# Differential attention on one core: the group's output copy moves from ScalarE to VectorE, and two row buffers become one

## The chip, the core and the metric

One core of a Trainium2 chip runs the whole kernel. A core has five engines that work through queues of their own, each in its order: TensorE (PE in the profile; its weight loads are PEld), VectorE (DVE), ScalarE (ACT), GpSimd (POOL) and SyncE (SP, which here only issues DMA transfers). An instruction that must wait for another engine holds up everything behind it in its own queue. The metric is the device time of one execution in microseconds; lower is better.

## The reference

One layer of a hybrid diffusion backbone: a modulated norm, one input projection into queries, keys, values and Fourier channels, then attention on one half of the heads and Fourier mixing on the other, an output projection, and an MLP. What this case touches is the differential attention of the 2048 latent tokens (4 heads, 2560 keys) and what follows it:

```python
def diff_attention(q, k, v, lam):
    ...
        s = jnp.einsum('bqhmd,bkhmd->bhmqk', qblk, k).astype(jnp.float32) * scale
        p = jax.nn.softmax(s, axis=-1)
        a = p[:, :, 0] - lam * p[:, :, 1]
        return jnp.einsum('bhqk,bkhe->bqhe', a.astype(v.dtype), v)
...
def merge(attn, four, subln_g, lam_init, w_out):
    a = rms_norm(attn, subln_g) * (1.0 - lam_init)
    return jnp.concatenate([a.reshape(b, n, ATTN_WIDTH), four], axis=-1) @ w_out
```

So each head has two softmax maps (m = 0 and 1), their difference weights the values, and each token's 128 outputs per head are divided by their root mean square before the output projection.

## The kernel before

The program runs in stages: setup and input projection with the Fourier part (to about 550 us), attention (to about 1255 us), output projection (to about 1470 us), and the MLP (to the end). In attention the latent queries are cut into groups of 256 (class `Group`): 8 groups per head, 4 heads, 32 groups, counted here from 0 to 31 in order of time. A smaller class `Prompt` does the 256 context tokens of each head in between.

A group has four softmax steps, one for each half j of its 128 queries and each map m. A step has five blocks of 512 keys:

- `fill`: TensorE makes one block of scores (tile Ss, in PSUM; two matmuls). The five PSUM banks for Ss are shared by all steps, so a block of the next step can be filled only when the exponential of a block of this step has read its bank.
- `rowmax`: VectorE takes the maximum of each row of the block (L1086); `comb` joins the five maxima (L1089).
- `exp`: ScalarE takes exponentials (L1105) into P0s or P1s.
- `combine`: GpSimd scales P1s (L1120) and adds it to P0s (L1121).

Six steps later the weights are transposed by TensorE (`tr`, tile pts), copied and split by ScalarE (`ah`, tile ahs, L1143) and VectorE (`al`, tile als, L1148), and multiplied with the values into one PSUM bank named po (`mul`, L95 to L97). When a group's last product is in po, a chain of small steps finishes it:

- `o1` copies po to oTs in SBUF (L1173).
- `oq` squares it on ScalarE into osqs (L1177); `o2` sums the squares on TensorE (tile pss, L1182); `o5` on VectorE and `opow` on GpSimd make one factor per token.
- `o6` stores these factors to DRAM, `o7` loads them back as rows on all partitions (tile rbs, L1201).
- `o8` on GpSimd multiplies oTs by rbs (L1206), and `o9` stores the result (att, L1210).

The order of all this is written out by hand: every call of every group gets a time in a table, and the calls are issued in the order of these times, so each engine's queue follows it. In units of one step, `o1` stands 11.2 steps after a group's first, amid the exponentials of a later group; `oq` 1.7 steps after `o1`, `o8` 4.8 and `o9` 5.4 steps after it. A group begins every four steps, so in the table `o8` of group k comes 0.9 steps before `oq` of group k+1.

A tile's tag names a place, and `bufs` says how many places the tag has. A new tile waits until the last user of the place is done. In the kernel before, oT has 2 places, osq has 1 and rb has 1. The last group (31) has places of its own in another pool.

The output projection begins directly behind the last products on TensorE. Its first tiles are made by ScalarE (woh) and VectorE (wol, mh, ml).

Of the kernel before, what the change touches and what calls it, by code (L numbers as in the profile page):

```python
# [11 lines left out]
F32 = mybir.dt.float32  # L12
# [7 lines left out]
P = 128  # L20
# [21 lines left out]
def body(tc, a, out):  # L42
    nc = tc.nc
    ctx = ExitStack()
    with ctx:
# [944 lines left out]
        with ExitStack() as c3_:  # L990
# [49 lines left out]
            class Group:  # L1040
# [128 lines left out]
                    nc.tensor.matmul(self.po[:, 0:P], self.hd.vf[kb][:, 0, :], self.A[kb][0][:, 0:P], start=False, stop=False)  # L1169

                def o1(self):
                    self.oT = self.op.tile([P, 256], F32, tag="oT", name=f"oT{self.nm}", bufs=1 if self.last else 2)
                    nc.scalar.copy(self.oT, self.po[:, 0:256])  # L1173

                def oq(self):
                    self.osq = self.op.tile([P, 256], F32, tag="P1_1" if self.hd.s else "osq", name=f"osq{self.nm}", bufs=1)
# [20 lines left out]

                def o7(self):
                    q, n = self.place()
                    self.rb = self.op.tile([P, 256], F32, tag="P0_1" if self.hd.s else "rb", name=f"rb{self.nm}", bufs=2 if self.hd.s else 1)  # L1200
                    q.dma_start(self.rb, rsd[self.hd.h][n:n + 1].partition_broadcast(P).rearrange("p o d -> p (o d)"))  # L1201

                def o8(self):
# [925 lines left out]
```

## Time and profile before

| what | value |
|---|---|
| time, median of 3 runs | 2867.51 us (2867.2 to 2867.67) |
| the profiled execution | 2865.04 us, its span 2863.3 us |
| granted TensorE clock, mean | 0.998 |
| VectorE busy | 1982.4 us (69%) |
| ScalarE busy | 1525.3 us (53%) |
| GpSimd busy | 1068.7 us (37%) |

The profile is one execution. Its span is the time from the first to the last instruction; the 1.7 us between span and time lie around it. The profiled execution was 2.47 us shorter than the median. A busy share is an average over stages with different limits, so the attention stage has to be read by itself. In the views, a row "615.12 0.37 ACT L1173 COPY oTs<-po" is an instruction by its start, its duration, engine, line, operation, and the tiles out<-in; what stands in square brackets behind it is the idle time of its engine just before it and what ended that.

### The profile page before, as it was taken

Reading aid. Unit: us, or ns where it says so; the run is one execution under the profiler, and the core shown is the slowest. Engines: PE = TensorE matmul, PEld = TensorE weight load, DVE = VectorE, ACT = ScalarE, POOL = GpSimd, SP = SyncE. Lnnn points to the kernel's source line nnn. Section 1 sums busy time; section 2 is a strip of 40 time slices with the busy share of each in tenths; the row PEclk is TensorE's granted clock in tenths of the full one; section 3 lists DMA queues with packets and bytes.
Section 4 is the critical chain, followed back from the end, with each engine's and each line's share of the span. In section 5 each row is a group of like instructions: output and inputs, shape, how many; then the busy total and the mean of one; then the engine's idle time right before and its main releaser. Section 6 shows DMA issues by size and latency. Waiting matters only on the chain.

```text
span 2863.3 us, 43138 instructions
## 1 busy us (share of the span) xinstructions
PE 2830.0 (99%) x15093; PEld 2462.1 (86%) x15093; DVE 1982.4 (69%) x3357; ACT 1525.3 (53%) x3383; POOL 1068.7 (37%) x855
## 2 busy tenths in 40 slices
PE   8999999999999999999999999999999999999999
PEld 5888888688888888888889999999998888888887
DVE  7777786888888888864477777778775354345554
ACT  4333332788888888853356565556555332333221
POOL 1221223789898898942223333333332000000000
PEclk9999999999999999999999999999999999999999
DMA  7777767431222322147767676667747464445663
GB/s 284 215 213 206 234 202 248 159 109 47 78 74 53 112 54 87 46 121 211 246 218 234 221 247 229 220 219 237 235 168 255 146 203 135 137 144 185 207 204 110
DMA packets 404795, 497.69 MB, mean 174 GB/s; under 512 B 31539, under 2 KB 320672, under 8 KB 401506
## 3 DMA queue, kind: packets, MB, share of 16 engines
q1 hardware_dynamic: 399088, 484.35, 53.4%
q0 software_dynamic: 1936, 7.41, 0.8%
q10 hardware_dynamic: 3554, 3.17, 0.3%
q8 instruction: 119, 1.95, 0.3%
q14 instruction: 98, 0.80, 0.1%
HBM read 317.30 MB, written 179.62 MB: 174 GB/s over the span
## 4 chain that ended last, share of the span: by engine, by line
PE 54%; DVE 1%; DMA 0%; issue 0%; ACT 0%; SPq 0%; POOL 0%; DVEq 0%; POOLq 0%
PE ps L95 8%; PE ps L97 8%; PE ps L96 8%; PE pB L1746 2%; PE pB L1745 2%; PE pB L1744 2%; PE pA L1744 2%; PE pC L1746 2%; PE pA L1745 2%; PE pC L1744 2%; PE pC L1745 2%; PE pA L1746 2%; PE po L97 2%; PE po L95 2%; PE po L96 2%; PE pD L1746 1%
## 5 line engine op out<-in xcount | busy, mean ns | idle before, releaser
L1086 DVE TENSOR_REDUCE mxs<-Ss 128x1 f32<-128x512 f32 x636 | 404.9, 685 | 85.5 <-PE Ss L1081 78.2
L1421 DVE TENSOR_TENSOR sl<-sr,sh 128x768 fp32r<-128x768 f32 x168 | 161.8, 964 | 331.6 <-ACT sh L1420 331.1
L1121 POOL TENSOR_TENSOR P0s<-P0s,P1s 128x1024 f32<-128x1024 f32 (+2 forms) x128 | 377.2, 2947 | 10.7
L1420 ACT CAST sh<-sr 128x768 fp32r<-128x768 f32 x168 | 140.6, 838 | 418.3 <-PE ps L96 418.3
L1786 POOL TENSOR_TENSOR gs<-g,g 128x384 f32<-128x384 f32 x48 | 69.7, 1453 | 469.3 <-ACT g L1756 426.4
L1105 ACT ACTIVATE P1s<-Ss,mxs 128x512 f32<-128x512 f32 x318 | 215.4, 694 | 47.7 <-DVE mxs L1089 43.9
L95 PE MATMUL pj<-wh,hh 128*128 128x512 f32 x576 | 228.9, 397 | 2.0 <-DVE hh L556 2.0
L95 PE MATMUL ps<-thT,sh 128*128 128x512 f32 x585 | 227.6, 389 | 0.0
L96 PE MATMUL ps<-tlT,sh 128*128 128x512 f32 x585 | 227.6, 389 | 0.0
L97 PE MATMUL ps<-thT,sl 128*128 128x512 f32 x585 | 227.6, 389 | 0.0
L96 PE MATMUL pj<-wl,hh 128*128 128x512 f32 x576 | 227.3, 395 | 0.1
L97 PE MATMUL pj<-wh,hl 128*128 128x512 f32 x576 | 225.8, 392 | 0.0
L1105 ACT ACTIVATE P0s<-Ss,mxs 128x512 f32<-128x512 f32 x318 | 214.6, 692 | 4.1 <-DVE mxs L1089 4.0
L1136 PE MATMUL pts<-ident,P0s 128*128 128x128 f32 x1280 | 193.4, 275 | 4.8 <-DVE als L1148 1.8
L1081 PE MATMUL Ss<-KS0s,Qs 128*128 128x512 f32 x636 | 188.8, 418 | 4.9 <-ACT P1s L1105 3.7
L1081 PE MATMUL Ss<-KS1s,Qs 128*128 128x512 f32 x636 | 188.1, 419 | 1.8 <-ACT P0s L1105 1.4
L1136 PEld LDWEIGHTS pts<-ident,P0s 128*128 128x128 f32 x1280 | 152.8, 142 | 36.3 <-issue 4.2
L1755 ACT ACTIVATE g<-uz 128x384 f32<-128x384 f32 x144 | 75.8, 526 | 200.2 <-DVE uz L1778 174.1
L1120 POOL TENSOR_SCALAR P1s<-P1s,tots 128x1024 f32<-128x1024 f32 (+2 forms) x128 | 171.5, 1340 | 5.8
L1148 DVE TENSOR_TENSOR als<-pts,ahs 128x512 fp32r<-128x512 f32 x256 | 163.7, 681 | 10.7 <-ACT ahs L1143 10.6
L1143 ACT CAST ahs<-pts 128x512 fp32r<-128x512 f32 x256 | 146.7, 607 | 40.9 <-PE pts L1136 40.9
L95 PE MATMUL ps<-ophT,sh 128*128 128x512 f32 x423 | 164.7, 389 | 1.1 <-DVE uz L1778 1.1
(536 smaller groups left out, 8012.8 us busy)
## 6 DMA issues: line engine op xcount, KB each, us to landing
sr<-sd SPq DMA_DIRECT2D x84, 768.0 KB, 4.3
a<-in_w SPq DMA_DIRECT2D x184, 256.0 KB, 3.6
sd<-gs SPq DMA_DIRECT2D x192, 192.0 KB, 1.9
sd<-g SPq DMA_DIRECT2D x144, 192.0 KB, 4.0
wm<-in_w_mod SPq DMA_DIRECT2D x32, 512.0 KB, 5.2
Qs<-qd SPq DMA_DIRECT2D x32, 512.0 KB, 5.1
b<-in_w SPq DMA_DIRECT2D x64, 256.0 KB, 4.9
b<-tsum SPq DMA_DIRECT2D x64, 256.0 KB, 4.6
```

What stands on the lines that cost most here:

```text
L95: nc.tensor.matmul(ps, lh, rh, start=first, stop=False)
L96: nc.tensor.matmul(ps, lh, rl, start=False, stop=False)
L97: nc.tensor.matmul(ps, ll, rh, start=False, stop=last)
L1081: nc.tensor.matmul(S[:, :w], self.Q[:, x, m, j * P:j * P + P], self.hd.KS[m][:, b * 512:b * 512 + w], start=(x == 0), stop=(x == 1))
L1086: nc.vector.tensor_reduce(self.mx[j][:, m, b:b + 1], self.S[j, m, b], axis=AX.X, op=ALU.max)
L1105: nc.scalar.activation(dst, S, AF.Exp, bias=self.mx[j][:, m, 6:7], accum_out=self.sm[j][:, m, b:b + 1])
L1120: nc.gpsimd.tensor_scalar(p, p, tot[:, 3:4], 0.0, op0=ALU.mult, op1=ALU.add)
L1121: nc.gpsimd.tensor_add(d, d, p)
L1136: nc.tensor.transpose(pt[:, c:c + P], self.p0[j][:, (kb + t) * P:(kb + t + 1) * P], ident)
L1744: nc.tensor.matmul(ps, wh[:, c], hh[:, k, :], start=first and k == 0, stop=False, skip_group_check=True)
L1745: nc.tensor.matmul(ps, wh[:, c], hl[:, k, :], start=False, stop=False, skip_group_check=True)
L1746: nc.tensor.matmul(ps, wl[:, c], hh[:, k, :], start=False, stop=k == 3, skip_group_check=True)
```

## The change

It edits two functions of `Group`. `o1` is issued on VectorE instead of ScalarE, and oT has three places instead of two. The tile rb loses its own place and takes the tag osq, which has one place: squares and factor rows of all groups but the last now use the same kilobyte of each partition in turn. (What the line `if self.hd.s` selects is for the context tokens, whose class has its own `o1`; for them nothing changes.)

```diff
                 def o1(self):
-                    self.oT = self.op.tile([P, 256], F32, tag="oT", name=f"oT{self.nm}", bufs=1 if self.last else 2)
-                    nc.scalar.copy(self.oT, self.po[:, 0:256])
+                    self.oT = self.op.tile([P, 256], F32, tag="oT", name=f"oT{self.nm}", bufs=1 if self.last else 3)
+                    nc.vector.tensor_copy(self.oT, self.po[:, 0:256])
...
                 def o7(self):
                     q, n = self.place()
-                    self.rb = self.op.tile([P, 256], F32, tag="P0_1" if self.hd.s else "rb", name=f"rb{self.nm}", bufs=2 if self.hd.s else 1)
+                    self.rb = self.op.tile([P, 256], F32, tag="P0_1" if self.hd.s else "osq", name=f"rb{self.nm}", bufs=2 if self.hd.s else 1)
```

The place of the call in the table is the same, so the queues of TensorE, GpSimd and SyncE keep their order. First place, VectorE in the loop: the queue around the copy of group 2 (als are the low halves of two transposed blocks, mxs the row maxima of the next step's first two score blocks).

```order
@@ -857,4 +859,5 @@
 L1148 TENSOR_TENSOR als_3_0_6429<-pts_3_0_6364,ahs_3_0_6404 128x512
 L1148 TENSOR_TENSOR als_3_2_6433<-pts_3_2_6391,ahs_3_2_6411 128x512
+L1173 COPY oTs_2_6447<-po 128x256
 L1086 TENSOR_REDUCE mxs_5_0_6441<-Ss_5_0_0_0_6444 128x1
 L1086 TENSOR_REDUCE mxs_5_0_6441<-Ss_5_0_0_1_6452 128x1
```

The copy now stands between the split of the weights and the first row maximum of the next step. At the same place ScalarE's queue loses it:

```order
@@ -453,5 +451,4 @@
 L1105 ACTIVATE P1s_4_1_0_6431,sms_4_1_6289<-Ss_4_1_1_0_6369,mxs_4_1_6288 128x512
 L1105 ACTIVATE P1s_4_1_0_6431,sms_4_1_6289<-Ss_4_1_1_1_6383,mxs_4_1_6288 128x512
-L1173 COPY oTs_2_6447<-po 128x256
 L1105 ACTIVATE P1s_4_1_1_6450,sms_4_1_6289<-Ss_4_1_1_2_6388,mxs_4_1_6288 128x512
 L1105 ACTIVATE P1s_4_1_1_6450,sms_4_1_6289<-Ss_4_1_1_3_6400,mxs_4_1_6288 128x512
```

It stood between the second and the third exponential of a step. Second place, ScalarE near the end of attention, around the squares of group 29 (osqs_5 of the last head). Here no instruction moves, but the semaphores that they wait for do. The kernel before:

```order
L1143 CAST ahs_6_10_14580<-pts_6_10_14569 128x512 [waits DVE_49,PE_49]
L1143 CAST ahs_6_12_14582<-pts_6_12_14574 128x512 [waits DVE_49,PE_49]
L1177 ACTIVATE osqs_5_14600<-oTs_5_14518 128x256 [waits Activation_49]
L1143 COPY ahs_6_14_14623<-pts_6_14_14610 128x512 [waits PE_49]
L1143 CAST ahs_6_16_14625<-pts_6_16_14618 128x512 [waits DVE_49,PE_49]
```

And the changed kernel:

```order
L1143 CAST ahs_6_10_14580<-pts_6_10_14569 128x512 [waits DVE_49,PE_49]
L1143 CAST ahs_6_12_14582<-pts_6_12_14574 128x512 [waits DVE_49,PE_49]
L1177 ACTIVATE osqs_5_14600<-oTs_5_14518 128x256 [waits DMAHW5_49,DVE_49,Pool_49]
L1143 COPY ahs_6_14_14623<-pts_6_14_14610 128x512 [waits PE_49]
L1143 CAST ahs_6_16_14625<-pts_6_16_14618 128x512 [waits DVE_49,PE_49]
```

Where the squares waited for ScalarE's own copy alone, they now wait for VectorE's copy, and for GpSimd and a DMA queue: the load of the factor rows of the group before into the shared place, and the multiplication `o8` of that group, which reads them. The same holds for every group from 1 to 30. Third place, VectorE at the end of attention:

```order
@@ -1904,4 +1935,5 @@
 L1148 TENSOR_TENSOR als_7_16_14805<-pts_7_16_14775,ahs_7_16_14782 128x512
 L1148 TENSOR_TENSOR als_7_18_14807<-pts_7_18_14784,ahs_7_18_14803 128x512
+L1173 COPY oTs_7_14825<-po 128x256
 L1547 SCALAR_TENSOR_TENSOR wol_0_14888<-wout_13376,cols,woh_0_14880 128x512
 L1573 CAST mh_14909<-wout_13378 128x1024
```

The copy of the last group (31), which needs the last product of the whole stage, now stands ahead of the first weight and input tiles of the output projection in VectorE's queue.

## The prediction

> **What bounds the kernel now.** I read the engines' busy lines first, then busy time by stage, the waits of TensorE in the attention loop, and the timeline of single steps.
>
> ```profile
> PE 2830.0 (99%) x15093; PEld 2462.1 (86%) x15093; DVE 1982.4 (69%) x3357; ACT 1525.3 (53%) x3383; POOL 1068.7 (37%) x855
> ```
>
> ```profile
> 550.00:1260.00 710.00, 701.54 (x4556) 601.56 (x4555) 590.65 (x1172) 613.26 (x1641) 626.65 (x470) 1.00 0.27 70
> ```
>
> The second row is the attention stage: window and length, busy time of TensorE, its weight loads, VectorE, ScalarE and GpSimd, then the clock. TensorE is nearly always busy, yet the other three run at 83 to 88% too, so each can hold it for fractions of a microsecond. The waits of weight loads between 575 and 1225 us show one that belongs to the copy:
>
> ```profile
> PEld Ss L1081 <- ACT P1s L1105: 16.0, 29, 0.6
> ```
>
> 29 times a score block waited for an exponential of P1s. 29 of the 32 copies (groups 0 to 28) stand in that loop. The timeline of one such step, group 2's copy:
>
> ```profile
> 613.60 1.28 DVE L1148 TENSOR_TENSOR als<-pts,ahs 128x512 fp32r<-128x512 f32 x2
> ...
> 614.42 0.28 PE L97 MATMUL po<-ahs,Vs 128*128 128x256 f32 x1
> 614.46 0.68 ACT L1105 ACTIVATE P1s<-Ss,mxs 128x512 f32<-128x512 f32 x1
> ...
> 614.89 1.18 PE L1081 MATMUL Ss<-KS0s,Qs 128*128 128x512 f32 x4
> ...
> 615.12 0.37 ACT L1173 COPY oTs<-po 128x256 f32<-128x256 f32 x1
> 615.37 0.71 ACT L1105 ACTIVATE P1s<-Ss,mxs 128x512 f32<-128x512 f32 x1
> 615.64 2.04 DVE L1086 TENSOR_REDUCE mxs<-Ss 128x1 f32<-128x512 f32 x3 [0.77 <-PE Ss L1081]
> ...
> 616.22 0.73 PE L1081 MATMUL Ss<-KS0s,Qs 128*128 128x512 f32 x2 [0.15 <-ACT P1s L1105]
> ...
> 617.90 1.29 DVE L1086 TENSOR_REDUCE mxs<-Ss 128x1 f32<-128x512 f32 x2 [0.21 <-PE Ss L1081]
> ```
>
> The chain: ScalarE copies at 615.12, its third exponential starts at 615.37 instead, TensorE's third score block waits for the bank until 616.22 (0.85 after that exponential's start), and VectorE's fourth maximum waits until 617.90.
>
> **The copy on VectorE.** Its duration is bounded by VectorE's other PSUM copies, with ScalarE's beside them:
>
> ```profile
> L1143 DVE COPY ahs<-pts 128x512 f32<-128x512 f32 x1 | 0.7, 692 | 0.4 <-PE pts L1136 0.4
> L118 DVE COPY cols<-pr 128x128 f32<-128x128 f32 x1 | 0.3, 291 | 0.6 <-PE pr L117 0.6
> L1173 ACT COPY oTs<-po 128x256 f32<-128x256 f32 x32 | 11.8, 370 | 4.7 <-DMA att<-oTs 4.2 <-PE po L97 0.6
> ```
>
> Between 0.29 us (128 columns) and 0.69 us (512), 256 columns lie at 0.42 us. The last product of po ends at 614.42 + 0.28 = 614.70 and the split at 614.88, so the copy fits into the 0.77 us in which VectorE idles anyway, and ends near 615.35, before the first maximum at 615.64. Cover needed: 0.42 of 0.77. Without it the maximum, and the whole step, moves by the difference.
>
> **Gain in the loop.** Without the copy the third exponential starts 0.25 us earlier. TensorE has filled two blocks by then: a matmul costs (1.64 - 1.18) / 2 = 0.23 us by the four above and the six below, so it is free at 614.89 + 0.91 = 615.80 and released at 615.97, 0.25 earlier. VectorE's maxima then follow without the 0.21 gap. The step is shorter by 0.21 to 0.25 us. In groups 5, 13 and 21 nothing waits, since sums of the context tokens stand ahead:
>
> ```profile
> 684.42 1.64 PE L1081 MATMUL Ss<-KS0s,Qs 128*128 128x512 f32 x6
> ...
> 685.16 3.13 DVE L1086 TENSOR_REDUCE mxs<-Ss 128x1 f32<-128x512 f32 x5 [0.89 <-PE Ss L1081]
> ```
>
> Six matmuls and five maxima run through. So 26 groups gain: 26 x 0.23 = 6.0 us (5.5 to 6.5). POOL and SP keep their queues; what is late next is VectorE's chain of five maxima.
>
> **The shared place in the loop.** The squares of group k+1 now wait on ScalarE for `o8` of group k on GpSimd; behind them stand the exponentials of P1s, and TensorE's sums pss wait for them. In the trace before, `o8` ends after the squares' start for k = 1, 2, 9, 10, 17 and 18 (by 1.09, 1.15, 0.93, 1.02, 1.66 and 1.67 us) and for k = 28; elsewhere before 29 it is done at least 1.09 us ahead. The first and the longest of the six:
>
> ```profile
> 623.69 0.46 ACT L1177 ACTIVATE osqs<-oTs 128x256 f32<-128x256 f32 x1
> 624.04 0.74 POOL L1206 TENSOR_TENSOR oTs<-oTs,rbs 128x256 f32<-128x256 f32 x1 [4.14 <-DMA rbs<-rs]
> 624.84 0.69 ACT L1105 ACTIVATE P1s<-Ss,mxs 128x512 f32<-128x512 f32 x1 [0.69 <-POOL oTs L1206]
> ...
> 626.18 0.69 ACT L1105 ACTIVATE P1s<-Ss,mxs 128x512 f32<-128x512 f32 x1
> 626.51 1.64 PE L1081 MATMUL Ss<-KS0s,Qs 128*128 128x512 f32 x6
> ...
> 985.54 0.46 ACT L1177 ACTIVATE osqs<-oTs 128x256 f32<-128x256 f32 x1
> 986.47 0.74 POOL L1206 TENSOR_TENSOR oTs<-oTs,rbs 128x256 f32<-128x256 f32 x1 [4.71 <-DMA rbs<-rs]
> ```
>
> The cover: ScalarE idles 0.69 us before the exponentials, and the third block, filled at 626.51 + 0.91 = 627.42, is released at 626.18 + 0.85 = 627.03, so 0.39 us more. Only what exceeds 1.08 us costs. With the waits of the trace that is 0.01 + 0.07 + 0.58 + 0.59, some 1.2 us. But the loop gains about 0.4 us on the load between two syncs, so all six grow; 0.4 on the first of each pair, 0.2 on the second gives 2.5 us, less some that VectorE's contiguous maxima hide. I take +1.5 (0.8 to 2.7).
>
> **The end of attention.** Here the same wait has no cover:
>
> ```profile
> 1231.64 0.43 ACT L1177 ACTIVATE osqs<-oTs 128x256 f32<-128x256 f32 x1
> ...
> 1233.17 0.50 PE L1182 MATMUL pss<-ones,osqs 128*128 128x1 f32 x4
> ...
> 1236.34 3.49 POOL L1121 TENSOR_TENSOR P0s<-P0s,P1s 128x1536 f32<-128x1536 f32 x1
> ...
> 1239.80 0.73 POOL L1206 TENSOR_TENSOR oTs<-oTs,rbs 128x256 f32<-128x256 f32 x1
> ...
> 1242.35 0.37 ACT L1173 COPY oTs<-po 128x256 f32<-128x256 f32 x1 [4.17 <-DMA att<-oTs]
> ...
> 1242.78 0.39 PE L95 MATMUL po<-ahs,Vs 128*128 128x256 f32 x1 [1.94 <-ACT oTs L1173]
> ```
>
> `o8` of group 28 stands in GpSimd's queue behind the last combines and ends at 1240.53. The squares of group 29 then end at 1240.96 instead of 1232.07, and TensorE's sums, in order, start near 1241.1 instead of 1233.17: +7.9. In return the hold at 1242.78 goes: group 30's copy waited there for the store of group 28, and with three places it needs that of group 27. Net +6.0. Then the clock:
>
> ```profile
> 1240.24:1243.65 3.41, 1.47 (x13) 1.23 (x12) 0.00 (x0) 1.30 (x4) 0.95 (x2) 1.00 0.23 74
> 1243.65:1247.06 3.41, 3.41 (x17) 3.32 (x17) 1.85 (x3) 1.46 (x4) 0.74 (x1) 0.50 0.13 41
> ```
>
> A stretch of 3.41 us with 1.94 idle was followed by one at half clock: 1.7 us lost, which goes with that hold. The new hold of 7.9 us contains a whole idle stretch, so TensorE restarts at half clock and stays there for the rest of one stretch plus a busy one, 3.4 to 6.8 us, or 1.7 to 3.4 lost, less the 1.7 saved: +0.85. This part is +6.8 (4.3 if no clock is lost anew; 7.7).
>
> **The last copy.**
>
> ```profile
> 1252.37 0.74 DVE L1547 SCALAR_TENSOR_TENSOR wol<-wout,cols,woh 128x512 fp32r<-128x512 f32 x1
> 1253.03 0.69 DVE L1573 CAST mh<-wout 128x1024 fp32r<-128x1024 f32 x1
> 1253.75 1.22 DVE L1574 TENSOR_TENSOR ml<-wout,mh 128x1024 fp32r<-128x1024 f32 x1
> ...
> 1254.44 0.39 PE L95 MATMUL po<-woh,mh 128*128 128x512 f32 x1
> 1254.64 0.37 ACT L1173 COPY oTs<-po 128x256 f32<-128x256 f32 x1 [0.57 <-PE po L97]
> 1255.03 0.50 PE L97 MATMUL po<-woh,ml 128*128 128x512 f32 x1
> ...
> 1259.87 0.69 DVE L1573 CAST mh<-mT 128x1024 fp32r<-128x1024 f32 x1 [0.43 <-DMA mT<-four]
> ...
> 1261.88 0.50 PE L97 MATMUL po<-woh,ml 128*128 128x512 f32 x1 [0.42 <-DVE ml L1574]
> ```
>
> Before, VectorE made wol, mh and ml while TensorE finished the last products. Now the copy stands ahead of them and can start only at 1254.64. The three begin at 1255.0 instead of 1252.37: 2.6 later, and TensorE's first product with ml too. VectorE's 0.43 idle before the next mh gives 0.4 back: +2.2. TensorE idles 1.7 + 0.6 us within about 3 us there, more than the 1.94 that halved the clock; whether it falls into one stretch depends on its phase, so I add two thirds of 1.7: +3.3 (2.2 to 3.9). I charge all this in full because TensorE is the bound behind it.
>
> **Sum.** -6.0 + 1.5 + 6.8 + 3.3 = +5.6 us. On the profiled execution's 2865.04 that is 2870.6; the median of the runs stood 2.47 above it, so 2867.51 + 5.6 = 2873.1. All ends together give +0.8 to +8.8, 2868.3 to 2876.3.
>
> **Rivals.** First, the other side: the hold at the end of attention does not come, because GpSimd reaches `o8` of group 28 early. Then -6.0 + 1.5 - 1.9 - 1.7 + 3.3 = -4.8, 2862.7. It decides once `o8` ends 5.6 us earlier, by 1234.9. Against it, GpSimd shows no idle ahead of the row at 1239.80.
>
> Second, the copy on VectorE does not fit its gap (over 0.77 us, or po late): no gain, 5.6 + 6.0 = +11.6, 2879.1. VectorE's even 512-column copy took 0.69, against this.
>
> Third, the short hold of the last copy leaves the clock alone, since its idle falls into two stretches: -6.0 + 1.5 + 6.8 + 2.2 = +4.5, 2872.0. The Trainium skill, TensorE: Matmul & The Clock Gate, section "Why this matters for your kernels", has a rule by which this always holds: only idle gaps over about 3 us throttle the clock. The trace differs: 1.94 us did.
>
> **How the numbers follow.** 0.2% is 5.7 us, about what a measurement can tell from no change. The forecast has 0.68: 0.34 above that bound, 0.34 below it, for its centre lies on it. The third rival has 0.19 (0.14 same, 0.05 slower), the first 0.07, the second 0.06. Faster 0.07, same 0.48, slower 0.45. The range 2868 to 2877 takes the forecast's ends and the third rival, and leaves out the other two.
>
> **What would show it.** Right: VectorE's copy of about 0.4 us with the gap of 0.21 before the fourth maximum gone; steps with a copy some 0.23 shorter; squares waiting for GpSimd six times by 1 to 2 us and once by about 9; TensorE idle some 8 us before the sums of group 29, with half clock behind it; no hold for att; mh and ml of the projection after the copy. Wrong: a first maximum delayed by the copy, fewer than six such waits, or a projection whose start does not wait for VectorE.

## The result and the profile after

The changed kernel takes 2871.43 us in the median (2868.37 to 2873.57, 22 runs), the kernel before, timed beside it, 2866.61 us (2864.74 to 2868.81, 22 runs): ratio 1.0016, 95% interval 1.0009 to 1.0023. In the two profiled executions the span went from 2863.3 to 2869.1 us. So the change costs some 5 us. The forecast was 2873.1, with +5.6 for the change.

The page after, its span and busy times:

```profile
span 2869.1 us, 43149 instructions
PE 2831.6 (99%) x15093; PEld 2465.4 (86%) x15093; DVE 1991.9 (69%) x3389; ACT 1516.1 (53%) x3351; POOL 1069.7 (37%) x855
```

VectorE has 32 instructions more than before and ScalarE 32 fewer. To see where the time went, three marks divide each span: the first of the short maxima of line 1089 in group 0, the same in group 31, and the first product of the MLP (line 1744). From that last one to the end every kernel of this study takes 1395.1 us. "Loop" below is the time from the first mark to the second, "tail" from the second to the third.

| | loop | tail |
|---|---|---|
| before | 687.09 | 260.43 |
| after | 681.34 (-5.75) | 271.70 (+11.27) |

The loop became shorter and the tail longer by twice as much. (The marks sum to +5.52; the loop also began 0.32 later after.)

**The loop.** The timeline of group 2's copy, after:

```profile
613.57 1.28 DVE L1148 TENSOR_TENSOR als<-pts,ahs 128x512 fp32r<-128x512 f32 x2
...
614.76 0.42 DVE L1173 COPY oTs<-po 128x256 f32<-128x256 f32 x1
614.82 1.84 PE L1081 MATMUL Ss<-KS0s,Qs 128*128 128x512 f32 x6
...
615.09 0.69 ACT L1105 ACTIVATE P1s<-Ss,mxs 128x512 f32<-128x512 f32 x1
615.57 1.89 DVE L1086 TENSOR_REDUCE mxs<-Ss 128x1 f32<-128x512 f32 x3 [0.38 <-PE Ss L1081]
...
617.61 1.29 DVE L1086 TENSOR_REDUCE mxs<-Ss 128x1 f32<-128x512 f32 x2 [0.15 <-PE Ss L1081]
```

VectorE's copy fills half of the idle time before the first maximum: that was 0.77, and 0.38 is left. TensorE runs six score products through where it did four and two. The first three maxima take 1.89 in place of 2.04, and the gap before the fourth is 0.15 in place of 0.21. The step with the copy is 5.42 us long where it was 5.70. The copies by line, after (nanoseconds, shortest, median and longest), and the waits of weight loads that answer to the row shown of before:

```profile
L1173 DVE COPY oTs<-po x32: 412/416/426, 570.2 to 1255.9; 128x256 f32<-128x256 f32 x32
```

```profile
PEld Ss L1081 <- ACT P1s L1105: 12.3, 43, 0.4
```

The waits for an exponential of P1s are shorter (0.4 us at the longest in place of 0.6, 12.3 in all in place of 16.0), though they come 43 times now, not 29. So that the 29 waits of before equalled the 29 copies of that stretch was no sign that each wait belonged to a copy.

**The squares.** ScalarE's waits over the whole attention, after (us in total, times, longest); before there was no row of the first kind:

```profile
ACT osqs L1177 <- POOL oTs L1206: 16.9, 7, 8.6
ACT osqs L1177 <- DVE oTs L1173: 1.0, 1, 1.0
```

Six of the seven waits stand in the loop (0.71, 1.14, 1.53, 1.50, 1.89 and 1.53 us, groups 2, 3, 10, 11, 18 and 19). The seventh, 8.6 us, is that of group 29 in the tail:

```profile
1230.83 3.42 POOL L1121 TENSOR_TENSOR P0s<-P0s,P1s 128x1536 f32<-128x1536 f32 x1
1234.20 0.73 POOL L1206 TENSOR_TENSOR oTs<-oTs,rbs 128x256 f32<-128x256 f32 x1
1234.96 0.42 ACT L1177 ACTIVATE osqs<-oTs 128x256 f32<-128x256 f32 x1 [8.62 <-POOL oTs L1206]
1235.43 0.80 PE L1182 MATMUL pss<-ones,osqs 128*128 128x1 f32 x3 [7.51 <-ACT osqs L1177]
```

Behind the last combine of the row GpSimd multiplies group 28's output, then ScalarE's squares may overwrite the factor rows, then TensorE goes on after 7.51 us without work.

**The last copy.** Timeline at the start of the projection, after:

```profile
1255.87 0.42 DVE L1173 COPY oTs<-po 128x256 f32<-128x256 f32 x1 [2.19 <-PE po L97]
...
1256.87 0.69 DVE L1573 CAST mh<-wout 128x1024 fp32r<-128x1024 f32 x1
1257.59 1.23 DVE L1574 TENSOR_TENSOR ml<-wout,mh 128x1024 fp32r<-128x1024 f32 x1
...
1257.70 0.47 PE L95 MATMUL po<-woh,mh 128*128 128x512 f32 x1 [1.87 <-DVE mh L1573]
...
1258.87 0.80 PE L97 MATMUL po<-woh,ml 128*128 128x512 f32 x1 [0.35 <-DVE ml L1574]
```

VectorE idles 2.19 us for the last product of `po`, then copies, and only then makes mh; TensorE waits 1.87 us for it.

**The clock.** Busy time by engine (PE, PEld, DVE, ACT, POOL) in stretches of 3.41 us, then the granted clock, the share of the DMA engines and GB/s; after:

```profile
1227.41:1230.82 3.41, 0.51 (x5) 0.31 (x3) 0.69 (x1) 0.00 (x0) 3.25 (x3) 1.00 0.04 2
1230.82:1234.23 3.41, 0.00 (x0) 0.00 (x0) 0.00 (x0) 0.00 (x0) 3.40 (x2) 0.50 0.00 0
1234.23:1237.65 3.42, 2.22 (x11) 2.22 (x12) 0.16 (x1) 0.63 (x2) 1.40 (x3) 0.50 0.21 66
1237.65:1241.06 3.41, 3.41 (x18) 3.41 (x17) 1.38 (x2) 1.55 (x3) 0.73 (x1) 0.50 0.17 51
...
1254.72:1258.13 3.41, 1.54 (x12) 1.20 (x10) 2.23 (x4) 2.38 (x5) 0.00 (x0) 1.00 0.48 98
1258.13:1261.55 3.42, 3.07 (x11) 2.25 (x9) 3.42 (x6) 3.42 (x7) 1.10 (x1) 0.50 0.93 261
1261.55:1264.96 3.41, 3.41 (x9) 2.70 (x9) 3.38 (x6) 1.79 (x4) 3.37 (x2) 0.50 1.01 409
```

Both holds are followed by half clock: 10.24 us from within the first, of which TensorE has 5.63 of work, and 6.83 us behind the second. Before, there was one stretch of 3.41 in this part of the kernel.

### The profile page after: what moved, and what is told of

The parts are those of the page before. It is cut to its first block, busy times and chain, and to the rows that moved or that the text cites. A ratio compares the mean times of both kernels' runs of the same rounds, so it can differ in the third digit from the quotient of the medians.

```text
span 2869.1 us, 43149 instructions
## 1 busy us (share of the span) xinstructions
PE 2831.6 (99%) x15093; PEld 2465.4 (86%) x15093; DVE 1991.9 (69%) x3389; ACT 1516.1 (53%) x3351; POOL 1069.7 (37%) x855
## 4 chain that ended last, share of the span: by engine, by line
PE 53%; DVE 1%; DMA 0%; issue 0%; ACT 0%; SPq 0%; POOL 0%; DVEq 0%; POOLq 0%
PE ps L95 8%; PE ps L96 8%; PE ps L97 8%; PE pB L1746 2%; PE pB L1744 2%; PE pB L1745 2%; PE pC L1745 2%; PE pC L1744 2%; PE pA L1745 2%; PE pA L1746 2%; PE pA L1744 2%; PE pC L1746 2%; PE po L97 2%; PE po L96 2%; PE po L95 2%; PE pD L1746 1%
```

## The experiments

Theory: four terms, a gain in the loop, waits of the squares in the loop, the hold in the tail, the last copy with the clock behind it. The rivals are named with each run. All were timed in rounds beside the kernel before, whose median was 2866.33 to 2866.89 in them.

### One part of the change at a time

`e_loop_copy`, edit to the kernel before:

```diff
-nc.scalar.copy(self.oT, self.po[:, 0:256])
+(nc.vector.tensor_copy if self.hd.h < H - 1 or self.g < 5 else nc.scalar.copy)(self.oT, self.po[:, 0:256])
```

> The kernel before, with the copy of groups 0 to 28 on VectorE and nothing else changed (groups 29 to 31 stay on ScalarE, two output places, factor rows with a place of their own). Four-term theory: a step with a copy is 0.28 us shorter in the trace after (5.42 for 5.70), in 26 groups, so -7.3 us, some 2859.3 beside 2866.6 before (ratio 0.9975), and group 31's scores start about 7 us earlier. Rival (the loop was shortened by the third output place, not by the engine of the copy): within 1.5 us of before. Rival (the copy also costs VectorE where it has no idle): -2 to -5.

Measured: 2859.51 us beside 2866.47, ratio 0.9973 (0.9962 to 0.9984); loop 679.48 (-7.61), tail 261.26 (+0.83). It is the engine of the copy that shortens the loop, not the third place, and VectorE's copy costs nothing beside it: neither rival holds. Step by step (from one short maximum to the next), 24 of the 29 steps with a copy became 0.26 to 0.29 us shorter, that of group 7 0.55, and those of groups 1, 5, 13 and 21 kept their length; together this is 7.2 of the 7.6 us.

`e_share_only`, edit to the changed kernel:

```diff
-nc.vector.tensor_copy(self.oT, self.po[:, 0:256])
+nc.scalar.copy(self.oT, self.po[:, 0:256])
```

> The changed kernel with all copies back on ScalarE: three output places and the shared place of squares and factor rows remain. Four-term theory: in the loop the waits of the trace before beyond 1.08 us, some 1.2 us; at the end TensorE's sums of group 29 held some 7.5 us, less the hold for a store that goes (1.9), plus some clock: +6 to +7.5. Together +7 to +9, some 2874.5 (ratio 1.0028). Rival (the shared place only moves a wait, the cost lies in VectorE's last copy and the clock after it): 0 to +2.

Measured: 2873.54, ratio 1.0023 (1.0014 to 1.0032); loop 687.18 (+0.09), tail 267.46 (+7.03). The tail of its timeline:

```profile
1239.42 0.73 POOL L1206 TENSOR_TENSOR oTs<-oTs,rbs 128x256 f32<-128x256 f32 x1
1240.19 0.42 ACT L1177 ACTIVATE osqs<-oTs 128x256 f32<-128x256 f32 x1 [8.68 <-POOL oTs L1206]
...
1240.66 1.01 PE L1182 MATMUL pss<-ones,osqs 128*128 128x1 f32 x4 [7.57 <-ACT osqs L1177]
```

The shared place costs 7 us, all of it at the end. The rival (0 to +2) is out. In the loop it costs next to nothing here (0.09), against the 1.2 that was expected: the four waits (4.3 us in all) are covered.

`e_last_copy`, edit to the kernel before:

```diff
-nc.scalar.copy(self.oT, self.po[:, 0:256])
+(nc.vector.tensor_copy if self.last else nc.scalar.copy)(self.oT, self.po[:, 0:256])
```

> The kernel before, with the copy of the last group alone on VectorE. Four-term theory: first product of the projection 1.9 to 2.2 us later, and half clock behind the idle time: +1.9 to +4.5 in all, likeliest +3.5 (ratio 1.0012). Rival (the clock takes no part, what the trace after shows of it varies from run to run): +1.9 to +2.2. Rival (VectorE catches up on its lateness within the projection's first row): 0 to +1.

Measured: 2869.76, ratio 1.0009 (1.0000 to 1.0018), that is +3.3 by the medians; loop -0.17, tail 264.97 (+4.54). The wait for mh is 1.87 us, as after. In this trace the stretch with that wait has 1.54 of 3.41 us busy, as after, and the next two are at half clock:

```profile
1252.90:1256.31 3.41, 1.54 (x13) 1.37 (x13) 1.98 (x4) 2.47 (x6) 0.00 (x0) 1.00 0.23 59
1256.31:1259.72 3.41, 3.27 (x10) 2.12 (x9) 3.41 (x5) 3.41 (x7) 0.00 (x0) 0.50 0.73 124
1259.72:1263.14 3.42, 3.42 (x10) 2.74 (x10) 3.38 (x7) 2.06 (x4) 1.90 (x2) 0.50 0.99 345
```

From the projection's first product to that of the MLP, before and in this run:

```profile
1254.44:1468.15 213.71, 212.62 (x1006) 176.26 (x1005) 112.11 (x162) 79.91 (x189) 56.17 (x55) 1.00 0.74 229
1256.13:1472.41 216.28, 215.34 (x1004) 178.67 (x1005) 112.68 (x162) 78.10 (x186) 55.51 (x55) 0.98 0.72 226
```

So in these two traces the 4.5 has two parts: the first product comes 2.0 us later (48.69 for 46.71 behind group 31's first short maximum), and behind it TensorE is busy 2.7 us longer with the same products, while its idle time stays (0.94 for 1.09). The second part is the half clock. VectorE does not catch up.

`e_tail_own`, edit to the changed kernel:

```diff
-"P0_1" if self.hd.s else "osq"
+"P0_1" if self.hd.s else "rb" if self.hd.h == H - 1 and self.g in (4, 5, 6) else "osq"
```

> The changed kernel, with a place of their own for the factor rows of groups 28, 29 and 30 alone; the others still share. Four-term theory: the hold of 7.5 us before the sums of group 29 goes with its half clock, and the hold for a store (1.9, and 1.7 of clock) stays away: 9 to 11 us under the changed kernel, 3 to 6 under the one before, some 2862 (ratio 0.9983). Rival (the cost lies in the last copy and its clock): within 2 us of the changed kernel, 2870 to 2872.

Measured: 2862.91, ratio 0.9987 (0.9978 to 0.9996), 8.5 us under the 2871.43 of the changed kernel; tail 262.36, 9.3 less than after. By the medians that is just under the 9 to 11 expected. So the hold before the sums of group 29 is what makes the changed kernel slower. The loop, 682.34, still has six of the squares' waits.

### What is left when the parts are taken out

`e_last_act`, edit to the changed kernel:

```diff
-nc.vector.tensor_copy(self.oT, self.po[:, 0:256])
+(nc.scalar.copy if self.last else nc.vector.tensor_copy)(self.oT, self.po[:, 0:256])
```

> The changed kernel, with the copy of the last group back on ScalarE. Four-term theory: the projection's first product no longer waits 1.9 us for mh and no half clock follows; the last copy alone cost 4.5 us in the trace where it was the only change, so 3.5 to 5 under the changed kernel, some +1.3 over the one before (2867.9, ratio 1.0005). Rival (TensorE, held 7.5 us before, is late anyway, so the wait for mh hides something that then comes up, as ScalarE's woh): 0 to 2 under the changed kernel, 2869.5 to 2871.5.

Measured: 2868.25, ratio 1.0006 (0.9997 to 1.0015), 3.2 us under the changed kernel by the medians (3.5 when each is taken against the kernel before of its own rounds), at the lower edge of the 3.5 to 5 expected; tail 267.37, 4.33 less than after. The term adds to that of the hold; nothing came up behind it.

`e_all_own`, edit to the changed kernel (the last group still shares its place):

```diff
-"P0_1" if self.hd.s else "osq"
+"P0_1" if self.hd.s else "osq" if self.last else "rb"
```

> The changed kernel, with a place of their own for the factor rows of all groups but the last, which shares; three output places and VectorE's copies stay. Four-term theory with the first four runs: group 31 starts 7.6 us earlier than before (no wait of squares in the loop, which cost 1.9 in the changed kernel and 2.9 in the run with a place for the end alone), and the tail stands as in that run, +1.9: -5.7 (-4.5 to -7), some 2860.8 (ratio 0.9980). Rival (the loop's waits for GpSimd are covered and the 1.9 is scatter of the DMA): as the run with a place for the end alone, 2862.9.

Measured: 2860.62, ratio 0.9980 (0.9971 to 0.9988); loop 679.86 (-7.23), tail 263.07. The loop is back at that of the loop's copy alone. From group 8 to group 31, the four kernels that share the place with VectorE's copies need 514.9, 515.8, 515.4 and 515.3 us (after, `e_tail_own`, `e_last_act`, `e_fill`); the five that do not share need 513.0 to 513.6 (`e_loop_copy`, this one and the three below with "best" in their names). So the waits in the loop cost 1.9 us, and cost it only with the faster loop.

`e_best` takes both edits, of `e_all_own` and `e_last_act`.

> The same with the copy of the last group on ScalarE: every term that cost is taken out, the gain in the loop is kept. Four-term theory: -7.6 in the loop, the hold for a store (1.9) and its clock (up to 1.7) gone, nothing for the last copy: -9 to -11, 2856 to 2858. Rival (at the end ScalarE's woh is the next bound, for which TensorE waited 2.5 us in the run with a place for the end alone, so what is taken out there gives little): -7 to -8.5, 2858 to 2859.5.

Measured: 2860.34, ratio 0.9978 (0.9969 to 0.9987); loop 679.70 (-7.39), tail 262.13 (+1.70). Not 9 to 11 faster, but 6.5, less than the rival has, too. The hold for a store is gone, and the tail is still no shorter than before: the projection's first product comes 1.0 us earlier behind group 31's first short maximum (45.72 for 46.71), and from there to the MLP it takes 2.7 us longer (216.40 for 213.71), with 6.83 us of half clock in it. The run with that hold removed alone shows the same.

Beside `e_all_own` it gains 0.3 us, within the scatter: there VectorE's last copy (at 1245.58) delays nothing, because mh, at 1247.34, still waits 0.68 us for the load of its input. So in these runs the last copy cost its 3 to 4 us only where that load had landed before the copy was done.

`e_places` is `e_best` with all copies on ScalarE, so that of the change only the third output place is left (and the last group's shared place).

> Three output places and a place of their own for the factor rows (the last group's excepted), all copies on ScalarE: of the change, the third output place alone. Term of the prediction (the hold for a store, 1.9, and 1.7 of clock go): -3.6, 2863.3 (ratio 0.9987). Rival (the projection's first input, loaded behind the stores of the prompt, is only 0.7 us ahead of TensorE before, so what goes at the hold comes back as a wait for mh, with half clock behind it): the first product of the projection some 1 us earlier after group 31's start, and in all -1 to +1, 2866 to 2868.

Measured: 2868.30, ratio 1.0004 (0.9995 to 1.0012); loop 687.11 (+0.02), tail 262.07 (+1.64). No gain, where the prediction's own term would have it at -3.6. The rival's mechanism is borne out, though at +2.0 beside 2866.33 the kernel is slower than its -1 to +1: the projection's first product comes 0.8 us earlier (45.90 for 46.71 behind group 31's first short maximum), and 6.83 us of half clock follow the wait. Its timeline (SPq rows are the queue's own):

```profile
1240.21 0.75 POOL L1206 TENSOR_TENSOR oTs<-oTs,rbs 128x256 f32<-128x256 f32 x1
1240.99 0.32 SPq L1210 DMA_DIRECT2D att<-oTs  x1
1241.41 0.37 SPq L1201 DMA_DIRECT2D rbp<-rs  x1
1244.90 0.75 POOL L1206 TENSOR_TENSOR oTp<-oTp,rbp 128x256 f32<-128x256 f32 x1 [3.28 <-DMA rbp<-rs]
1245.67 0.32 SPq L1210 DMA_DIRECT2D att<-oTp  x1
1246.40 2.77 SPq L1201 DMA_DIRECT2D rbs<-rs  x1
1250.02 0.37 SPq L1286 DMA_DIRECT2D wout<-att  x1
...
1253.26 0.69 DVE L1573 CAST mh<-wout 128x1024 fp32r<-128x1024 f32 x1 [3.45 <-DMA wout<-att]
...
1254.10 0.47 PE L95 MATMUL po<-woh,mh 128*128 128x512 f32 x1 [2.80 <-DVE mh L1573]
```

TensorE comes 2.8 us early and waits for mh, mh for the load of line 1286, which reads what the store of the prompt's output (`oTp`) has written, and so on up to GpSimd's `o8` of group 28. By the order of these rows that chain hangs on GpSimd, not on TensorE. Counted from group 31's first short maximum, mh starts at 45.30 before, and at 45.12, 45.06, 44.89, 45.16 and 45.12 in `e_loop_copy`, `e_places`, `e_best`, `e_best_fill` and `e_best_mix`. Before, TensorE's first product stood 0.7 us behind the end of mh; more than that cannot be had there.

### The clock, and the load

`e_fill`, edit to the changed kernel, ahead of the sums (`o2`) of group 29 alone:

```diff
+for r in range(fill): nc.tensor.matmul(ps[:, 256:512], self.hd.KS[0][:, 0:P], self.hd.KS[0][:, 0:256], start=True, stop=True)
```

(The line that matters is shown; `fill` is 56 for group 29 and 0 for all others, and `ps` is the whole bank of the sums.)

> The changed kernel, with 56 products of the resident keys written into unused columns of the bank of the sums, ahead of the sums of group 29: TensorE works (some 6.5 us) while it would idle, the wait itself stays, and no result uses these products. Clock theory: no half clock from 1231 to 1241, so the 5.6 us that TensorE worked at half clock behind the hold shrink by some 2.8: first product of the projection 19.5 us after the sums' start instead of 22.3, in all 1.5 to 3 us under the changed kernel. Rival (the clock costs nothing there, since other engines are waited for): within 0.7 us of the changed kernel. Rival (the filling delays the sums): slower by up to 1.5.

Measured: 2869.28, ratio 1.0006 (0.9998 to 1.0015), 2.2 us under the changed kernel by the medians; the single executions of the two overlap widely (2867.0 to 2872.19 and 2868.37 to 2873.57), so the times alone do not exclude the first rival. In the trace its tail is 269.95, 1.75 less than after:

```profile
1230.55 6.86 PE L1181 MATMUL pss<-KS0s 128*128 128x256 f32 x56
...
1237.97 0.42 ACT L1177 ACTIVATE osqs<-oTs 128x256 f32<-128x256 f32 x1 [8.84 <-POOL oTs L1206]
...
1238.44 0.61 PE L1182 MATMUL pss<-ones,osqs 128*128 128x1 f32 x4 [1.03 <-ACT osqs L1177]
```

The wait of the squares is as long as after (8.84 and 8.62), the clock stays at 1.00 until 1259.35, and from the sums' start to the projection's first product it takes 1258.65 - 1238.44 = 20.21 us where it took 1257.70 - 1235.43 = 22.27. So half clock behind the hold cost 2.1 us there. (In this trace and in that of `e_last_act` half clock also fell on the start of the loop, near 542 us, behind waits that the other traces have without it; its loop is 684.37, 3.0 longer than after, so its span is not shorter.)

`e_best_fill` is `e_best` with 20 transposes ahead of the projection's first product:

```diff
-po = PS[i, hf]
+po = PS[i, hf]; [nc.tensor.transpose(po[:, 0:P], ident, ident) for _ in range(FILL.pop() if FILL else 0)]
```

(`FILL` is a list with the one number 20.)

> The kernel with every costly term taken out (own places, last copy on ScalarE), and 20 transposes of the identity into the first bank of the projection ahead of its first product, whose results are overwritten: TensorE works for 2.3 of the 2.6 us in which it waits there for mh. Clock theory: no half clock behind it (6.8 us in that kernel's trace), -2 to -3.4 beside it, 2857 to 2858.5, with the wait as it was. Rival (the clock costs nothing there because VectorE's and ScalarE's splits are late anyway): within 0.7 of 2860.3.

Measured: 2861.49, ratio 0.9981 (0.9972 to 0.9989): not faster than `e_best` (2860.34), and not within the rival's 0.7 of it either. The clock theory as expected there falls, though the half clock itself did go from that place:

```profile
1244.26 2.34 PE L1584 MATMUL po<-ident 128*128 128x128 f32 x20
...
1247.25 0.47 PE L95 MATMUL po<-woh,mh 128*128 128x512 f32 x1 [0.65 <-DVE mh L1573]
...
1255.25 0.69 DVE L1573 CAST mh<-mT 128x1024 fp32r<-128x1024 f32 x1 [2.42 <-DMA mT<-four]
...
1256.09 0.47 PE L95 MATMUL po<-woh,mh 128*128 128x512 f32 x1 [1.75 <-DVE mh L1573]
```

TensorE went through the first row at full clock, then waited 1.75 us for the next row's input, and that wait was followed by half clock in turn (1258.12 to 1261.53). From the projection's first product to the MLP's TensorE is busy 0.7 us less than in `e_best` (214.59 for 215.33) and idle 2.6 us more (3.63 for 1.07). In these runs a clock that is kept was worth something where TensorE was late, as in `e_fill`, and nothing where it then met the next late load.

`e_best_mix`, edit to `e_best`, which puts the load of line 1286 ahead of the load of group 29's factor rows in SP's queue:

```diff
-add(base + (AVS - 2) * T + 0.7 * u, mix0_load)
+add(base + (AVS - 3.35) * T, mix0_load)
```

> The kernel with every costly term taken out, and the load of the projection's first input put ahead of the load of group 29's factor rows in SP's queue. Theory (TensorE's 2.6 us wait for mh is a wait for this load): the load is issued 2 to 2.5 us earlier, the wait shrinks to under 0.7, no half clock follows, -3 to -5 beside that kernel, 2855.5 to 2857.5. Rival (the load waits for the landing of the prompt's store, not for the queue): 0 to -1, 2859.5 to 2860.3. Rival (ScalarE's woh is next): the wait moves to woh, -1 to -2.5.

Measured: 2861.90, ratio 0.9985 (0.9976 to 0.9994), no gain over `e_best`:

```profile
1238.39 0.32 SPq L1210 DMA_DIRECT2D att<-oTp  x1
1243.18 0.37 SPq L1286 DMA_DIRECT2D wout<-att  x1
1243.64 0.46 SPq L1201 DMA_DIRECT2D rbs<-rs  x1
...
1246.87 0.63 PE L95 MATMUL po<-woh,mh 128*128 128x512 f32 x1 [2.89 <-DVE mh L1573]
```

With nothing between them in the queue the load still issues 4.8 us after the store, and TensorE waits 2.89. So it was not the queue's order. The queue's own waits from 1225 to 1262 us name what it was, the store of the prompt's output (us in total, times, longest):

```profile
SPq L1286 <- DMA att<-oTp: 4.4, 1, 4.4
```

The releaser is read from semaphores; the trace has no landing time for that store. At 2861.90 the kernel is slower than all three theories said. In its trace the load of the next input (mT from four) issues later, 49.24 us behind group 31's first short maximum where it was 46.56 in `e_best`, and the second mh starts at 55.53 in place of 53.77.

The fastest in these runs is the smallest change, the copies of the loop on VectorE and nothing else: 2859.51, 0.9973 of the kernel before (0.9962 to 0.9984); its interval overlaps those of `e_all_own` and `e_best`. `e_best` differs from it mainly in the store's hold, which it does not have, and gains nothing by that.

## Why the prediction was right, and where it was not

**The sum.** +5.6 was said, +5.84 measured between the two profiled spans and +4.8 between the medians. That the sum came so close is in part luck, for two misses of over 1 us cancel: the loop came out at -5.75 where the two terms for it gave -4.5, and the tail at +11.27 where the two terms gave +10.1. The number 2873.1 lies 1.7 above the median also because the three runs of before that it was built on stood 0.9 above the later 2866.61.

**The copy on VectorE.** Right: 32 copies at 0.416 us in the median (0.42 said), and it fits its gap. The second rival is out.

**Loop gain.** Mis-sized: -6.0 (5.5 to 6.5) said, -7.6 in `e_loop_copy`, 0.28 per step in place of 0.23. The step that failed is the one that took the gap of 0.21 before the fourth maximum for the whole. That gap did not go, 0.15 of it stayed; but the row of the first three maxima, 2.04 us where three back to back take 1.89, held another 0.15 of waiting that went as well, and the first maximum starts 0.04 earlier behind the split. These make 0.25 of the 0.28. That groups 5, 13 and 21 gain nothing was right; group 1 gains nothing either, and group 7 twice as much, and why these two differ is not shown.

**The shared place in the loop.** +1.5 (0.8 to 2.7) said, 1.9 measured, with six waits of 0.7 to 1.9 us. The argument that the faster loop makes the waits longer than their cover is borne out more sharply than it was put: with ScalarE's copies they cost 0.1, where the prediction's own working gave 1.2 from the trace before. (With the longer waits, 0.4 on the first and 0.2 on the second of each pair, its working adds up to 2.8 and not to the 2.5 that it states; the 1.5 taken was set below both.)

**The end of attention.** +6.8 said, +7.03 in `e_share_only`. The hold is 7.5 us (7.9 said). The clock term, 2.55 for the new hold, is 2.1 by `e_fill`. But one step stood on a false ground: the hold for the store of group 28 was credited with 1.9 us and 1.7 of clock. Taken away alone (`e_places`) it gives nothing, since mh is ready only 0.7 us ahead of TensorE; had the prediction been asked for the third place alone, it would have been wrong by 3.6 or more. In the changed kernel the credit is right in the sum, but the third place does not earn it: the store of group 28 lands at 1236.69 there, and the copy of group 30 starts at 1244.63, so by this trace the copy would not have waited with two places either. The new hold makes TensorE so late that the old one falls inside it. (No run has the shared place with two output places.)

**The last copy.** +3.3 (2.2 to 3.9) said; by the medians +3.3 (`e_last_copy`) and 3.2 (`e_last_act` against the changed kernel), by the profiles 4.5 and 4.3. The waits are 1.87 and, for ml, 0.35 us (1.7 and 0.6 were said). The profiles are higher because both show half clock for two stretches, not one, which cost 2.7 us in `e_last_copy`, where the prediction weighed one at two thirds and added 1.1. The executions of `e_last_copy` scatter from 2867.4 to 2873.0; that the clock makes this scatter is likely, not shown.

**The rivals.** The first (no hold, because GpSimd is early) is out: TensorE had been idle for 7 us when `o8` of group 28 ended at 1234.93. The mark that the prediction set for this rival, `o8` done by 1234.9, was all but reached, and the hold came even so: the faster loop had moved the copy of group 29 by 5.8 us as well (1221.08 for 1226.86), so GpSimd gained next to nothing on the squares that wait for it. Such a mark has to be set against the waiting instruction, not against the start of the program. The third (the clock stays whole behind the last copy) is out: in the three profiled executions with such a wait, after, `e_last_copy` and `e_fill`, half clock follows it for 6.83 us each time. The Trainium skill, TensorE: Matmul & The Clock Gate, section "Why this matters for your kernels", asks for gaps of over about 3 us; the trace differs again, one gap of 1.87 us was enough.

## What to carry to other kernels

When two buffers become one, list every pair of the old users on different engines and look up, for each iteration, how far apart they run; the loop may hide all of them and one iteration at the end, behind a long queue of another engine, may cost more than the loop gains. Price a removed wait by what is ready next: where the following input was ready 0.7 us ahead, taking out a hold of 1.9 us brought the next product forward by 0.8 (`e_places`), and nothing was left of that at the end. Two holds in a row on one engine need not add up: a longer one in front can swallow the one behind it. An instruction that moves to another engine is to be followed into the last iteration too, where the engine already has other work in front of it.

## What the runs showed of the hardware

Half clock comes in stretches of 3.41 us or whole multiples of it (3.41, 6.83 and 10.24 here), and within one trace their starts lie whole multiples apart: before, at 31.92 and 1243.65, 355 times 3.4133 us. So there is a fixed grid, and a gap's length alone does not decide. The hold for the store of 1.94 us before was followed by half clock; that of 1.89 in `e_loop_copy`, with nearly all of it in one stretch, by full clock, and the stretch held 1.62 us of work where that of before held 1.47 and that of after, behind the last copy, 1.54:

```profile
1234.36:1237.77 3.41, 1.62 (x14) 1.62 (x15) 0.66 (x2) 1.84 (x4) 0.18 (x1) 1.00 0.24 77
1237.77:1241.19 3.42, 3.42 (x30) 3.32 (x29) 1.92 (x4) 1.39 (x3) 0.74 (x1) 1.00 0.22 40
```

Between 1200 and 1300 us the work in a stretch tells the two apart in all these traces: half clock after 1.56 us (`e_best_fill`, 1254.71 to 1258.12) and less, full clock after 1.62 and more. It is no general border: near 540 us, at the start of the loop, stretches with 1.67 (`e_last_act`) and 1.83 (`e_fill`) were followed by half clock and one with 1.58 (`e_last_act`) by full clock. What else counts there is not shown.

```profile
538.83:542.24 3.41, 1.67 (x7) 0.77 (x6) 3.01 (x8) 3.41 (x11) 3.33 (x3) 1.00 0.01 2
```

The Trainium skill, TensorE: Matmul & The Clock Gate, section "What's actually happening", has a free-running window of 3413 ns, and the lengths seen here agree with it. How much work a stretch at half clock must hold before full clock returns stays open: 3.41 us was enough in `e_best_fill` (1258.12 to 1261.53) and not in `e_tail_own` (1250.50 to 1253.91).
